# A two-layer decoder trunk on one core: gate and up products through DRAM scratch, weight parts for two chunks, and weight sums made by accumulating transfers

## The chip, the cores and the metric

The kernel runs on one core of a Trainium2 chip. The metric is the device time of one execution in microseconds (us), lower is better. The core has a matrix engine (TensorE, "PE" in the profile), a vector engine (VectorE, "DVE"), a scalar engine (ScalarE, "ACT"), GpSimd ("POOL") and SyncE ("SP"), which here only issues transfers. Every engine works through its own instructions in order and waits on semaphores for the others. Sixteen DMA engines move the data that SP, ACT and POOL ask for.

## The reference, cut to what matters

Two layers work on 512 positions of 1024 features. Each has a mixer (attention with forget gates and a short convolution in the first, a gated linear recurrence in the second), a cross attention into 256 memory rows, and a SwiGLU block. Each part has the form x = x + norm(f(norm(x))). The change touches the SwiGLU block, whose width is 2816:

```python
D_FF = ((8 * D_MODEL // 3 + 255) // 256) * 256       # 2816
def swiglu(h, w_gu, w_down):
    g, u = jnp.split(h @ w_gu, 2, axis=-1)
    return (jax.nn.silu(g) * u) @ w_down
...
        h = rmsnorm(x, g_ffn_pre[layer])
        y = swiglu(h, w_ffn_gu[layer], w_ffn_down[layer])
        x = x + rmsnorm(y, g_ffn_post[layer])
```

Everything is float32.

## The kernel before, in words

**Split operands.** A float32 product is made from three matmuls of a rounded kind (`mm3`, L278). Each operand is split in a high part, a copy in the rounded type made by ACT, and a low part, the difference, made by DVE (`split_out`, L427, with the two instructions at L430 and L431). The three matmuls are high by high, high by low, low by high (L279 to L281). So each weight tile has to be loaded by SP (`load_raw`, L117), cast on ACT and subtracted on DVE before PE can use it.

**Buffers.** A buffer is a slot of a pool. `gpool` has 14 groups of 128 x 2048 elements. The raw weights (tag "st"), the high parts ("wh") and the low parts ("wl") have four buffers each of 128 x 1024 elements. Eight small buffers of 516 columns serve everything else of that kind (`sbuf`).

**The block.** `ffn` (L717) works in chunks of 256 columns of the weights, eleven for the gate and eleven for the up half. The first of each (`ws_gemm_split`, L334) is a plain product, woven with the end of the cross attention; its instructions go over the first 256 positions and then over the second. The other ten pairs use a Winograd form of the Strassen product (class `Winograd`, L353): the activations are cut into four blocks, by positions (halves) and by features (halves), the weight chunk into four blocks as well, and seven products replace eight. The activation side (`__init__`, L360) makes four sums once, splits them and keeps them in four groups "wa"; three further products use parts of the transposed activations, the groups "hTh" and "hTl", directly.

**The weight side** (`weights`, L381) runs for every chunk. It loads the upper half of the rows, r0, and the lower half, r1, each 128 x 4 x 256. Four sums on DVE at L384 make a third tile tt, a small tile t2, and overwrite half of r0. Then four splits follow: r0 (for the products "b11" and "t1"), t2, tt ("t4" and "t3") and r1 ("b21" and "b22"). With r0, r1 and tt a chunk holds three of the four "st" buffers, and its splits take four "wh" and four "wl".

**Products and outputs.** `gemm` (L396) runs the seven products in the order a11 b11, s2 t2, n1 t1, n3 t3, a12 b21, a22 t4, n4 b22, each 4 x 3 matmuls of 256 columns, 84 in all, and combines the results on DVE (L411, and through `out` L741 and L746). The gate chunk writes to one half of the PSUM banks and gets a Silu on ACT (L743); the up chunk uses the other half, and its result times the gate's is y (L748). Each pair of chunks makes 128 x 2 x 512 elements of y. Two pairs share a group "y2", so six groups hold all of y.

**The down projection** (`OutProj`, L439) contracts the 22 blocks of y with `w_ffn_down`. Its first half (`half0_steps`, L458) goes through the blocks two at a time: `parts` (L754) splits a pair's y, called two steps ahead, and a load and split of two weight rows follow. The second half (`half1`) uses the same split y again.

**What sets the order.** PE's instructions run as written. On the other engines and queues, the planner of the framework orders the instructions when the program is built: by program order as priority, by the time at which it reckons that inputs and buffers are there. It also places every wait. What it puts on one engine or queue runs in that order on the chip. SP's queue carries all weight loads; POOL's carries small work of the norms (the power at L210, `rstd`) and a few transfers.

Of the kernel before, what the change touches and what calls it, by code (L numbers as in the profile page):

```python
# [42 lines left out]
def trunk_kernel(ctx: ExitStack, tc: tile.TileContext, a: dict, out: bass.AP):  # L43
# [207 lines left out]
    def new_hT():  # L251
# [3 lines left out]
        ft.ghi, ft.glo, ft.raw = hi, lo, None  # L255
        return ft

    def put_T(hT, t, hs, bank=bankB):
        for hf in range(2):
            ps = bank()  # L260
            for j in range(4):
                nc.tensor.transpose(
                    out=ps[:, j * P:(j + 1) * P], in_=hs[hf][:, j * P:(j + 1) * P], identity=ident
                )
            v = ps.rearrange("p (k c) -> p k c", k=4)
            sl = slice(t * P, (t + 1) * P)
            if hT.raw:
                nc.scalar.copy(out=hT.raw[hf][:, :, sl], in_=v)
            last = (
                nc.scalar.copy(out=hT.ghi[hf][:, :, sl], in_=v).ins,  # L270
                nc.vector.tensor_tensor(
                    out=hT.glo[hf][:, :, sl], in0=v, in1=f(hT.ghi[hf][:, :, sl]), op=ALU.subtract
                ).ins,
            )
        return last

# [57 lines left out]
    def ws_gemm_split(w, c0s, hT, hook):  # L334

        wss = [w_chunk(w, c0) for c0 in c0s]
        banks = [[bankA() for _ in range(2)] for _ in c0s]
        for half in range(2):
            cols = slice(half * 256, half * 256 + 256)
            for i, ws in enumerate(wss):  # L340
                for m in range(2):
                    for kh in range(2):
                        wh, wl = ws[kh]
                        for kk in range(4):
                            k = 4 * kh + kk
                            ms = slice(m * P, (m + 1) * P)
                            mm3(banks[i][m][:, cols], wh[:, kk, ms], wl[:, kk, ms],
                                hT.hi[k][:, cols], hT.lo[k][:, cols], k == 0, k == KT - 1)
                    if half == 0:
                        hook(2 * i + m)  # L350
        return banks

    class Winograd:  # L353
# [6 lines left out]
        def __init__(self, hT):  # L360
            r0, r1 = hT.raw
            e, l = slice(0, 256), slice(256, 512)
            a21, a11, a22, a12 = r0[:, :, e], r0[:, :, l], r1[:, :, e], r1[:, :, l]
            sub = lambda o, i0, i1: nc.vector.tensor_tensor(out=o, in0=i0, in1=i1, op=ALU.subtract)
            self.parts = {}
            sub(a22, a21, a22)
            sub(a21, a21, a11)
            sub(a11, a11, a22)
            for name, raw in (("s2", a11), ("n1", a22), ("n3", a21)):
                self.put(name, raw)  # L370
            sub(a12, a12, a11)
            self.put("n4", a12)
            for name, hf, sl in (("a11", 0, l), ("a12", 1, l), ("a22", 1, e)):
                self.parts[name] = hT.ghi[hf][:, :, sl], hT.glo[hf][:, :, sl]

        def put(self, name, raw):
            g = group("wa")
# [1 line left out]
            split_out(raw, *self.parts[name])  # L379

        def weights(self, w, c0):  # L381
            r0, r1 = load_raw(w, 0, 4, c0, 256), load_raw(w, 4, 4, c0, 256)
            one, two = slice(0, P), slice(P, 2 * P)
            add = lambda o, i0, i1: nc.vector.tensor_tensor(out=o, in0=i0, in1=i1, op=ALU.add)  # L384
            t2 = sbuf("t2").rearrange("p (k c) -> p k c", k=4)
            tt = wst.tile([P, 4, 256], F32, tag="st", name="st")
            add(tt[:, :, two], r0[:, :, two], r1[:, :, two])
            add(t2, tt[:, :, two], r0[:, :, one])
            add(r0[:, :, two], r0[:, :, one], r0[:, :, two])
            add(tt[:, :, one], t2, r1[:, :, one])  # L390
            w1, w2 = split_w(r0, 4, 256), split_w(t2, 4, P)
            w3, w4 = split_w(tt, 4, 256), split_w(r1, 4, 256)
            return {"b11": (w1, one), "t1": (w1, two), "t2": (w2, one), "t4": (w3, one),
                    "t3": (w3, two), "b21": (w4, one), "b22": (w4, two)}

# [321 lines left out]
    def ffn(layer, hT, prev, proj):  # L717
        w = a["w_ffn_gu"][layer]
        y = Feat([None] * NFF, [None] * NFF)

        y2 = {}

        def y_rows(jp):

            if jp % 2 == 0:
                y2[jp // 2] = f(group("y2"))
            return y2[jp // 2][:, jp % 2 * 2:jp % 2 * 2 + 2, :]

        def act(jp, gb, ub):
            y_ = y_rows(jp)  # L730
            for m in range(2):
                s = sbuf("sw")
                nc.scalar.activation(out=s, in_=gb[m], func=AF.Silu)
                nc.vector.tensor_tensor(out=y_[:, m, :], in0=s, in1=ub[m], op=ALU.mult)

        def act_wino(jp, wino):

# [12 lines left out]
            wino.gemm(w, jp * 256, bankB, gate)  # L750
            y_ = y_rows(jp)
            wino.gemm(w, FF + jp * 256, bankA, up)

        def parts(jp):  # L754
# [388 lines left out]
    for layer in range(2):  # L1143
# [49 lines left out]
```

## Time and profile before

| | |
|---|---|
| median of three runs | 1481.75 us (1480.46 to 1481.83) |
| the profiled execution | 1479.13 us |
| its span, first to last instruction | 1477.3 us |
| granted TensorE clock | 0.998 |
| bytes moved | 151.26 MB, 102 GB/s over the span |
| weight loads of the gate and up stage | 88 of 512 KB |
| the weight sums at L384 | 160, from 383.0 to 1339.4 us |

In the rows of the profile a name such as wl<-st,wh tells what is written from what is read, by the program's names for tiles; t is the small sum t2, y also stands for the groups y2. A row of a group ends with the busy time, the mean of one in ns, and the idle time of the engine just before these instructions with what ended most of it. In a row of waits the engine that waited stands left of the arrow, what it waited for on the right. A row of single instructions begins with its start and its duration in us, and ends with the idle time before it, in brackets, where there was some. Matmuls overlap, so their single durations add up to more than PE's busy time.

### The profile page before, as it was taken

The numbers are of one execution on the slowest core, as the hardware profiler recorded it, in microseconds if no ns is written. First come the engines' busy times: TensorE is split into PE (matmuls) and PEld (weight loads), VectorE is DVE, ScalarE is ACT, GpSimd is POOL, SyncE is SP. The second block draws the span as 40 slices with busy tenths as digits, with TensorE's granted clock in tenths as the row PEclk, the third lists the DMA queues.
The fourth block names the chain that finished last, engine by engine and source line by source line (L and its number), as shares of the span: only waits on it lengthen the run. The fifth ranks groups of instructions, "written<-read, shape, count | busy, mean of one in ns | idle before, by whom it ended". The sixth has DMA issues, their size and how long they took to land. (4 is left out here: it accounts for less than half of the span.)

```text
span 1477.3 us, 21423 instructions
## 1 busy us (share of the span) xinstructions
PE 1423.2 (96%) x8564; PEld 1254.8 (85%) x8564; DVE 1021.3 (69%) x1623; ACT 660.8 (45%) x1069; POOL 37.6 (3%) x82
## 2 busy tenths in 40 slices
PE   8999999999998899999999999999999999989998
PEld 6777789888898888888889888988889888888886
DVE  5785767544888888883447998744588888888232
ACT  4354555434553433461334886543464333345130
POOL 1000000000100000000000000000010000000000
PEclk9999999999999999999999999999999999999999
DMA  5532253520322323233413236342122232234221
GB/s 174 180 100 79 79 178 108 163 75 23 112 72 86 100 86 101 86 126 115 156 53 94 86 100 193 124 155 72 31 85 72 86 96 92 86 100 130 99 86 57
DMA packets 119391, 151.26 MB, mean 102 GB/s; under 512 B 6182, under 2 KB 88178, under 8 KB 119291
## 3 DMA queue, kind: packets, MB, share of 16 engines
q1 hardware_dynamic: 114722, 140.92, 30.3%
q10 hardware_dynamic: 3896, 6.86, 1.6%
q0 software_dynamic: 672, 2.11, 0.4%
q8 instruction: 67, 1.10, 0.3%
q14 instruction: 34, 0.27, 0.1%
HBM read 147.76 MB, written 2.11 MB: 101 GB/s over the span
## 5 line engine op out<-in xcount | busy, mean ns | idle before, releaser
L431 DVE TENSOR_TENSOR wl<-st,wh 128x1024 fp32r<-128x1024 f32 x268 | 324.1, 1223 | 225.2 <-ACT wh L430 223.2
L430 ACT CAST wh<-st 128x1024 fp32r<-128x1024 f32 x268 | 277.9, 1050 | 425.2 <-DVE st L384 193.9
L279 PE MATMUL bA<-hTh,wh 128*128 128x256 f32 (+1 forms) x816 | 275.8, 338 | 0.0
L281 PE MATMUL bA<-hTh,wl 128*128 128x256 f32 (+1 forms) x816 | 272.3, 334 | 0.6 <-DVE wl L431 0.6
L280 PE MATMUL bA<-hTl,wh 128*128 128x256 f32 (+1 forms) x816 | 271.8, 333 | 0.0
L281 PEld LDWEIGHTS bA<-hTh,wl 128*128 128x128 f32 x816 | 154.9, 190 | 16.5 <-DVE wl L431 1.0
L280 PEld LDWEIGHTS bA<-hTl,wh 128*128 128x128 f32 x816 | 155.2, 190 | 13.7
L279 PEld LDWEIGHTS bA<-hTh,wh 128*128 128x128 f32 x816 | 155.1, 190 | 13.5
L281 PE MATMUL bB<-wa,wl 128*128 128x256 f32 x320 | 92.4, 289 | 22.8 <-DVE wl L431 22.8
L279 PE MATMUL bA<-wa,wh 128*128 128x256 f32 x320 | 92.5, 289 | 12.7 <-ACT wh L430 12.7
L281 PE MATMUL bA<-wa,wl 128*128 128x256 f32 x320 | 92.6, 289 | 4.5 <-DVE wl L431 4.5
L279 PE MATMUL bB<-wa,wh 128*128 128x256 f32 x320 | 90.5, 283 | 0.0
L280 PE MATMUL bB<-wa,wh 128*128 128x256 f32 x320 | 90.4, 283 | 0.0
L280 PE MATMUL bA<-wa,wh 128*128 128x256 f32 x320 | 90.4, 283 | 0.0
L281 PEld LDWEIGHTS bB<-wa,wl 128*128 128x128 f32 x320 | 61.2, 191 | 26.4 <-DVE wl L431 26.4
L456 PE MATMUL bB<-wh,y 128*128 128x512 f32 x208 | 81.1, 390 | 1.3 <-DVE y L431 1.3
L454 PE MATMUL bB<-wh,y 128*128 128x512 f32 x208 | 81.2, 390 | 1.1 <-ACT y L430 1.1
L455 PE MATMUL bB<-wl,y 128*128 128x512 f32 x208 | 80.9, 389 | 0.0
L279 PEld LDWEIGHTS bA<-wa,wh 128*128 128x128 f32 x320 | 61.2, 191 | 16.7 <-ACT wh L430 16.7
L281 PEld LDWEIGHTS bA<-wa,wl 128*128 128x128 f32 x320 | 61.2, 191 | 8.6 <-DVE wl L431 8.6
L281 PE MATMUL bB<-hTh,wl 128*128 128x256 f32 x240 | 68.0, 283 | 0.0
L279 PE MATMUL bB<-hTh,wh 128*128 128x256 f32 x240 | 67.9, 283 | 0.0
(289 smaller groups left out, 3143.4 us busy)
## 6 DMA issues: line engine op xcount, KB each, us to landing
st<-in_w_ffn_gu_dram SPq DMA_DIRECT2D x88, 512.0 KB, 3.5
st<-in_w_ffn_down_dram SPq DMA_DIRECT2D x44, 512.0 KB, 3.9
st<-in_w_xkv_dram SPq DMA_DIRECT2D x32, 512.0 KB, 5.0
st<-in_ab_w_in_dram SPq DMA_DIRECT2D x24, 512.0 KB, 3.7
st<-in_w_xq_dram SPq DMA_DIRECT2D x16, 512.0 KB, 3.5
st<-in_w_xo_dram SPq DMA_DIRECT2D x16, 512.0 KB, 3.8
st<-in_c_w_in_dram SPq DMA_DIRECT2D x16, 512.0 KB, 3.5
st<-in_ab_w_out_dram SPq DMA_DIRECT2D x8, 512.0 KB, 3.8
```

Source lines behind the costliest of these rows:

```text
L279: nc.tensor.matmul(out=ps, lhsT=wh, rhs=xh, start=first, stop=False)
L280: nc.tensor.matmul(out=ps, lhsT=wh, rhs=xl, start=False, stop=False)
L281: nc.tensor.matmul(out=ps, lhsT=wl, rhs=xh, start=False, stop=last)
L430: nc.scalar.copy(out=hi, in_=src)
L431: nc.vector.tensor_tensor(out=lo, in0=src, in1=f(hi), op=ALU.subtract)
L454: nc.tensor.matmul(out=ps, lhsT=yh, rhs=wh[:, kk, :], start=first, stop=False)
L455: nc.tensor.matmul(out=ps, lhsT=yh, rhs=wl[:, kk, :], start=False, stop=False)
L456: nc.tensor.matmul(out=ps, lhsT=yl, rhs=wh[:, kk, :], start=False, stop=last)
```

## The change

Five things change together.

- The sums of r0 with itself and of r0 with r1 are no longer made by DVE. A load on SP puts the block b12 into tt; an accumulating transfer on POOL adds b22 to it from DRAM, and another adds b11 to the second half of r0. The sums for t2 and for the first half of tt stay on DVE.
- r0 and r1 are loaded into one group, "wr", and their splits go to two groups, "wg". The splits of t2 and tt still use "wh" and "wl", of which a chunk now takes two each; of the "st" buffers it takes one.
- The products y go to a scratch tensor in DRAM, y2, written by SP (`put_y`) from an "st" buffer at the end of each pair, and read back into one by `parts` in the down projection.
- The transposed activations of this block are held in four groups by halves of features and of positions ("quads"), each with high and low parts, in place of two high and two low groups over all positions.
- `put_T` and `ws_gemm_split` address these quads through two small functions.

```diff
+    def new_quads():
+
+        ft = Feat(None, None)
+        ft.quads = [[group("hTq") for _ in range(2)] for _ in range(2)]
+        ft.raw = None
+        return ft
+
+    def dst_T(hT, hf, t):
+        if hT.hi:
+            sl = slice(t * P, (t + 1) * P)
+            return hT.ghi[hf][:, :, sl], hT.glo[hf][:, :, sl]
+        q, c = hT.quads[hf][t // 2], t % 2 * P
+        return q[:, :, c:c + P], q[:, :, 256 + c:256 + c + P]
+
+    def half_T(hT, k, half):
+        if hT.hi:
+            cols = slice(half * 256, half * 256 + 256)
+            return hT.hi[k][:, cols], hT.lo[k][:, cols]
+        q = hT.quads[k // 4][half][:, k % 4, :]
+        return q[:, 0:256], q[:, 256:512]
...
-            for name, hf, sl in (("a11", 0, l), ("a12", 1, l), ("a22", 1, e)):
-                self.parts[name] = hT.ghi[hf][:, :, sl], hT.glo[hf][:, :, sl]
+            for name, hf, half in (("a11", 0, 1), ("a12", 1, 1), ("a22", 1, 0)):
+                q = hT.quads[hf][half]
+                self.parts[name] = q[:, :, 0:256], q[:, :, 256:512]
...
         def weights(self, w, c0):
-            r0, r1 = load_raw(w, 0, 4, c0, 256), load_raw(w, 4, 4, c0, 256)
+            raw = f(group("wr")).rearrange("p a (b c) -> p (a b) c", c=256)
+            rows = w.rearrange("(k p) n -> p k n", p=P)
+            r0, r1 = raw[:, 0:4, :], raw[:, 4:8, :]
+            for kh, r in ((0, r0), (4, r1)):
+                nc.sync.dma_start(out=r, in_=rows[:, kh:kh + 4, c0:c0 + 256])
             one, two = slice(0, P), slice(P, 2 * P)
             add = lambda o, i0, i1: nc.vector.tensor_tensor(out=o, in0=i0, in1=i1, op=ALU.add)
             t2 = sbuf("t2").rearrange("p (k c) -> p k c", k=4)
-            tt = wst.tile([P, 4, 256], F32, tag="st", name="st")
-            add(tt[:, :, two], r0[:, :, two], r1[:, :, two])
+            tt = wst.tile([P, 4, 256], F32, tag="st", name="tt")
+
+            def split_g(r):
+                g = group("wg").rearrange("p a (b c) -> p (a b) c", c=256)
+                split_out(r, g[:, 0:4, :], g[:, 4:8, :])
+                return g[:, 0:4, :], g[:, 4:8, :]
+
+            nc.sync.dma_start(out=tt[:, :, two], in_=rows[:, 0:4, c0 + P:c0 + 2 * P])
+            nc.gpsimd.dma_start(out=r0[:, :, two], in_=rows[:, 0:4, c0:c0 + P], accum_op=ALU.add)
+            nc.gpsimd.dma_start(out=tt[:, :, two], in_=rows[:, 4:8, c0 + P:c0 + 2 * P], accum_op=ALU.add)
             add(t2, tt[:, :, two], r0[:, :, one])
-            add(r0[:, :, two], r0[:, :, one], r0[:, :, two])
             add(tt[:, :, one], t2, r1[:, :, one])
-            w1, w2 = split_w(r0, 4, 256), split_w(t2, 4, P)
-            w3, w4 = split_w(tt, 4, 256), split_w(r1, 4, 256)
+            w1, w2 = split_g(r0), split_w(t2, 4, P)
+            w3, w4 = split_w(tt, 4, 256), split_g(r1)
...
-        y2 = {}
+        y2 = dram.tile([P, NFF, 512], F32, name=f"y2_{layer}")
+        yraw = {}
 
         def y_rows(jp):
 
-            if jp % 2 == 0:
-                y2[jp // 2] = f(group("y2"))
-            return y2[jp // 2][:, jp % 2 * 2:jp % 2 * 2 + 2, :]
+            yraw[jp] = wst.tile([P, 2, 512], F32, tag="st", name="yr")
+            return yraw[jp]
+
+        def put_y(jp):
+            nc.sync.dma_start(out=y2[:, 2 * jp:2 * jp + 2, :], in_=yraw[jp])
...
             y_ = y_rows(jp)
             wino.gemm(w, FF + jp * 256, bankA, up)
+            put_y(jp)
 
         def parts(jp):
             yg = group("y")
-            src = y2[jp // 2][:, jp % 2 * 2:jp % 2 * 2 + 2, :]
+            src = wst.tile([P, 2, 512], F32, tag="st", name="yr")
+            nc.sync.dma_start(out=src, in_=y2[:, 2 * jp:2 * jp + 2, :])
             split_out(src, yg[:, 0:2, :], yg[:, 2:4, :])
...
-        hTf = new_hT()
+        hTf = new_quads()
```

More of the change, by code (lines that the diff above doesn't have):

```diff
@@ L268, in put_T @@
                 nc.scalar.copy(out=hT.raw[hf][:, :, sl], in_=v)
+            hi, lo = dst_T(hT, hf, t)
             last = (
[L270 to L273, printed above, removed]
+                nc.scalar.copy(out=hi, in_=v).ins,
+                nc.vector.tensor_tensor(out=lo, in0=v, in1=f(hi), op=ALU.subtract).ins,
             )
@@ L347, in ws_gemm_split @@
                             mm3(banks[i][m][:, cols], wh[:, kk, ms], wl[:, kk, ms],
-                                hT.hi[k][:, cols], hT.lo[k][:, cols], k == 0, k == KT - 1)
+                                *half_T(hT, k, half), k == 0, k == KT - 1)
                     if half == 0:
@@ L752, in act_wino @@
             wino.gemm(w, FF + jp * 256, bankA, up)
+            put_y(jp)
         def parts(jp):
             yg = group("y")
-            src = y2[jp // 2][:, jp % 2 * 2:jp % 2 * 2 + 2, :]
+            src = wst.tile([P, 2, 512], F32, tag="st", name="yr")
+            nc.sync.dma_start(out=src, in_=y2[:, 2 * jp:2 * jp + 2, :])
             split_out(src, yg[:, 0:2, :], yg[:, 2:4, :])
```

## The prediction

> **What bounds the kernel now.** I read the page's totals and its forty slices first, then a table of busy time in stretches, then the waits of the two stages that the change touches, then single instructions inside them.
>
> ```profile
> PE 1423.2 (96%) x8564; PEld 1254.8 (85%) x8564; DVE 1021.3 (69%) x1623; ACT 660.8 (45%) x1069; POOL 37.6 (3%) x82
> PE   8999999999998899999999999999999999989998
> DVE  5785767544888888883447998744588888888232
> DMA  5532253520322323233413236342122232234221
> ```
>
> TensorE (PE) is busy for 96% of the span, so 1477.3 - 1423.2 = 54 us is all that a change that leaves its matmuls alone can win. VectorE (DVE) runs at 8 tenths in two stretches, slices 10 to 17 and 29 to 36. These are the gate and up products of the two layers. In the table of stretches (columns: busy time and instructions of PE, weight load, DVE, ACT, POOL, then clock, DMA share, GB/s) I cut them into pieces of 23.33 us, which is one gate chunk plus one up chunk:
>
> ```profile
> 456.67:480.00 23.33, 20.91 (x168) 20.30 (x168) 19.64 (x31) 9.25 (x14) 0.00 (x0) 1.00 0.30 92
> 596.67:620.00 23.33, 21.19 (x173) 20.59 (x172) 19.51 (x31) 9.26 (x14) 0.00 (x0) 1.00 0.31 95
> 1203.33:1226.67 23.34, 21.20 (x173) 20.59 (x172) 19.63 (x31) 9.30 (x13) 0.00 (x0) 1.00 0.32 96
> 660.00:690.00 30.00, 30.00 (x134) 24.86 (x133) 14.39 (x13) 8.25 (x9) 0.00 (x0) 1.00 0.42 130
> ```
>
> Every pair loses 2.1 to 2.4 us of PE. Ten pairs in each of two layers make about 40 of the 54 us. The last row is the down projection: PE is full there. What PE waits for is in the waits of 370 to 640 us (first seven rows) and of 1060 to 1340 us (last three); columns are total, times, longest:
>
> ```profile
> ACT wh L430 <- DVE st L384: 97.1, 19, 5.8
> DVE wl L431 <- ACT wh L430: 18.3, 29, 2.4
> PE bB L281 <- DVE wl L431: 11.5, 9, 1.4
> PE bA L279 <- ACT wh L430: 5.7, 9, 0.7
> PE bA L281 <- DVE wl L431: 2.3, 10, 0.3
> SPq L119 <- DVE wx L411: 74.8, 16, 5.2
> SPq L119 <- DVE t L384: 66.4, 9, 7.4
> ...
> PE bB L281 <- DVE wl L431: 11.3, 9, 1.3
> PE bA L279 <- ACT wh L430: 5.7, 9, 0.7
> PE bA L281 <- DVE wl L431: 2.3, 10, 0.3
> ```
>
> (The two SPq rows are the transfer queue's own waits from 456 to 640 us.) PE waits for split weights only: 11.5 + 5.7 + 2.3 = 19.5 us in layer 0 and 11.3 + 5.7 + 2.3 = 19.3 us in layer 1, together 38.8 us. The casts wait for the weight sums of L384, and the loads wait for buffers that DVE has yet to release. One pair in single instructions:
>
> ```profile
> 480.02 0.38 PE L279 MATMUL bA<-wa,wh 128*128 128x256 f32 x1 [0.65 <-ACT wh L430]
> 480.75 0.39 PE L281 MATMUL bA<-wa,wl 128*128 128x256 f32 x1 [0.22 <-DVE wl L431]
> 492.61 0.39 PE L281 MATMUL bB<-wa,wl 128*128 128x256 f32 x1 [1.38 <-DVE wl L431]
> ...
> 485.46 0.68 DVE L384 TENSOR_TENSOR t<-st 128x512 f32<-128x512 f32 x1
> ...
> 490.67 1.29 DVE L748 TENSOR_TENSOR y<-y,sw 128x512 f32<-128x512 f32 x2
> 491.87 0.69 DVE L431 TENSOR_TENSOR wl<-t,wh 128x512 fp32r<-128x512 f32 x1
> ...
> 488.14 0.62 ACT L430 CAST wh<-t 128x512 fp32r<-128x512 f32 x1
> ```
>
> The late part is always the t2 weight of the second product: its low part at 491.87 us stands in DVE's queue behind the outputs of the chunk before, and PE goes on when it ends (491.87 + 0.69 = 492.56). DVE does 19.6 us in order in 23.3 us, with weights ready hardly ahead of their use.
>
> **The change, part by part.** 1. *Two sums fewer on DVE.* Each chunk makes four L384 sums; the change leaves t2 and tt.one.
>
> ```profile
> L384 DVE TENSOR_TENSOR st<-st x80: 680/685/694, 383.0 to 1332.8; 128x512 f32<-128x512 f32 x80
> ...
> L431 DVE TENSOR_TENSOR wl<-st,wh 128x1024 fp32r<-128x1024 f32 x268 | 324.1, 1223 | 225.2 <-ACT wh L430 223.2
> L430 ACT CAST wh<-st 128x1024 fp32r<-128x1024 f32 x268 | 277.9, 1050 | 425.2 <-DVE st L384 193.9
> ```
>
> The 80 st<-st are the removed ones (minimum, median, maximum in ns); the two page rows give the cast and the low part that every weight part needs. 80 x 0.685 = 54.8 us leave DVE, four per pair, 2.7 us: DVE goes from 19.6 to about 16.9 us per pair, 80% of PE's 21.2. DVE isn't the bound in itself; what this buys is room in its queue.
>
> 2. *Depth.* Before, wh and wl have four buffers and a chunk uses all four, and a chunk takes three of the four st buffers. Afterwards the two full parts of r0 and r1 go to the groups "wg", the raw weights to a group "wr", and t2 and tt alone take wh and wl, so four buffers hold two chunks. The groups suffice: of 14, three quads and four wa stay, 7 are left, and a chunk needs 3. The quad of a21, first half, is dead after the split products at the start, and the six groups of y2 are gone. A whole chunk (10.6 us of PE) of lead outweighs a stall of at most 1.4 us at a time. So the waits above go, except where there is no lead yet: the first chunks after the start of each layer, where DVE also makes the four wa parts. I leave 1 us per layer. Gain: 38.8 - 2 = 36.8 us.
>
> 3. *Transfers in place of the sums.* Per chunk they are one more load of 256 KB on SP and two accumulating ones of 256 KB on POOL; each is 128 x 4 rows of 512 B, so 512 packets. The trace has no accumulating transfer. The nearest rows (landing is the last column; the queue rows are of 456 to 480 us and, last, of 660 to 720 us):
>
> ```profile
> st<-in_w_ffn_gu_dram SPq DMA_DIRECT2D x88, 512.0 KB, 3.5
> cb<-cum POOLq DMA_DIRECT2D x8, 256.0 KB, 3.7
> L930 POOL DMA_DIRECT2D cb<-cum x8: 546/548/778, 66.0 to 147.3; - x8
> DMA to landing us min/median/max: 3.3/3.7/5.0
> q1 hardware_dynamic: 2112, 2.10, 28.2%
> q1 hardware_dynamic: 3536, 6.82, 36.5%
> ```
>
> The first queue row gives 0.282 x 24 x 16 engines / 2112 = 51 ns of an engine per packet of 1 KB, the second 0.365 x 60 x 16 / 3536 = 99 ns per 2 KB: time goes by bytes, so 512 B is some 26 ns. For an accumulating packet the low end is that, 26 ns; the high end is three whole 1 KB packets (read the source, read the target, write), 154 ns; I take 51 ns, two reads of 512 B, nearest to the row of 1 KB. Per pair: r0 and r1 2048 x 51 / 16 = 6.5 us; the tt loads 1024 x 26 / 16 = 1.7; the accumulating 2048 x 51 / 16 = 6.5 (3.3 to 19.7); the write of y 256 x 99 / 16 = 1.6. Sum 16.3 us of 21.2, from 13.1 to 29.5. So the engines keep up, at three quarters instead of 30%.
>
> The Trainium skill (DMA: Bandwidth & Descriptors, section "SDMA does more than copy") has the add unit combine two streams; two streams of 512 B would be my 51 ns, and no run here shows it yet. Against the change speaks its rule in "Rules for kernel authors" to make transfers of at least 1 MiB: by its fit of 2.0 us plus bytes over 436 GB/s a quarter MiB is 2.6 us, and with four accumulates one behind the other that would be an estimated 10.4 us per pair, still under PE's 21.2. The trace's own 256 KB transfer from POOL has 3.7 us.
>
> POOL issues 128 rows in 0.55 us; 512 rows take 0.55 to 2.2, four per pair 2.2 to 8.8 us of 21.2 on an engine that does nothing in this stage. Latency of the longest chain: load 3.5, issue up to 2.2, accumulate 3.7 to 5.0, cast 1.05, low part 1.22: 11.7 to 13 us. Raw weights of the chunk after next fit while a chunk runs, which is a lead of one to two chunks, 10.6 to 21 us. Cost 0; with the cover gone, each chunk waits for what is over.
>
> 4. *Products through DRAM.* Eleven writes and eleven reads of 512 KB per layer, all on SP's queue.
>
> ```profile
> out_dram<-x SPq DMA_DIRECT2D x8, 256.0 KB, 2.1
> st<-in_w_ffn_down_dram SPq DMA_DIRECT2D x44, 512.0 KB, 3.9
> 651.62 0.50 PE L454 MATMUL bB<-wh,y 128*128 128x512 f32 x1 [0.53 <-ACT y L430]
> 653.01 0.50 PE L456 MATMUL bB<-wh,y 128*128 128x512 f32 x1 [0.66 <-DVE y L431]
> ```
>
> The write waits for L748 on SP; behind it stand loads of chunks that PE wants a chunk later, so 0. A read per step of the down projection doubles the st buffers and bytes of half 0: 512 packets of 2 KB by 99 ns over 16 is 3.2 us in a step of 24 matmuls, 30.00 x 24 / 134 = 5.4 us. Landing 3.9, cast and low part 2.3 are 6.2 us per buffer, and four buffers over 6.2 us give 0.65 per us against 2 / 5.4 = 0.37 wanted. Hidden, too. The first reads ask for pairs 0 and 1, which were written over 200 us before; cost 0. If they had to wait for the last write: L748 0.69, write 2.1 to 3.9, read 3.9, cast and low part 2.3, 9 to 11 us after the last product, less the 1.2 us that PE waits there now, so 8 to 10 us per layer, 16 to 20 us. That is kept for the range.
>
> 5. *Quads and POOL's queue.* The split of each transposed tile is the same two instructions to other columns; 0. On POOL, the norms' power (L210) can stand behind an accumulate that waits for its load, at most 3.5 us per layer in the first chunk; I take 0 since PE has 24 us of split products there, and keep 7 us for the range.
>
> **Sum.** The profiled execution took 1479.13 us (span 1477.3), 2.6 us under the median 1481.75. 1479.1 - 36.8 = 1442.3, and 2.6 on top for the median makes 1445 us, 2.5% faster. With all 38.8 + 2 x 1.2 us of waits gone it is 1440.6. Runs differ by some 1.4 us, so the low end is 1438.
>
> **Rivals.** *A: accumulating transfers become the bound (slower).* Place: the 16 DMA engines in the gate and up stage. They decide once an accumulating packet costs more than (21.2 - 9.8) x 16 / 2048 = 89 ns; from (23.33 - 9.8) x 16 / 2048 = 106 ns the kernel is slower than before. At the 154 ns end a pair takes 29.5 us: 20 x (29.5 - 23.33) = +123 us, 1605 us; at 120 ns it takes 25.2 us, +37 us, 1519 us. For it: nothing in the trace prices such a packet. Against: the packets that it does show go by bytes.
>
> *B: the reads wait for the last write.* +16 to 20 us on the forecast, 1461 to 1465 us. For it: nothing shows how finely the order of transfers to the scratch tensor is kept. Against: the first reads name other rows of the scratch tensor than the last write.
>
> *C: the stalls are an order, not a depth.* The late low part of t2 was behind output instructions of DVE; its sum had been made at 485.46 us, six us before. If DVE's order keeps t2 behind those outputs, only the shorter queue helps: half of the waits, say 19 us, remain, 1464 us; with late accumulates ahead of DVE in addition nothing is won, 1482 us, and the change does not do what it says. For it: that row. Against: the cast it followed was at 488.14, limited by a chain that is now a chunk earlier.
>
> **How the numbers follow.** Forecast (1438 to 1453) 0.62; B or C with part of the gain (1453 to 1478) 0.15; C without gain 0.05; A or another loss 0.18. A difference of 0.2%, 3 us, is what a measurement of this kernel can tell from none. Faster 0.77, same 0.05, slower 0.18. The range goes from 1438 to 1488: forecast, B, C and the mildest part of A, about 0.82. The forecast's own range is 1438 to 1453.
>
> **What would show it.** Right: PE at 21 us of 21.2 to 21.6 per pair, no row of PE waiting for wl or wh beyond a few us, 40 and 40 L384 instead of 160, DVE near 80%, DMA share near 0.75 in the stage. Step 3 is wrong if ACT or DVE waits on transfers of gate and up weights stand at tens of us, or if the POOL transfers land after 10 us or more; A, if the DMA share is 9 tenths and PE's waits end in them. Step 4 is wrong if PE waits 8 us or more at the first matmul of the down projection. C, if PE's waits for wl are still there with weights long landed. My forecast falls if a pair takes more than 22 us.

## The result, and the profile after

The changed kernel takes 1597.41 us (median; 1592.17 to 1600.45). The kernel before, run beside it on the same chip, takes 1481.11 us (1479.89 to 1481.83). The ratio is 1.0782, with a 95% interval of 1.0748 to 1.0817: 7.8% slower, where 2.5% faster was forecast. The profiled execution has a span of 1598.1 us, 120.8 us more than the 1477.3 of before.

The page's totals and slices:

```profile
PE 1472.3 (92%) x8564; PEld 1297.9 (81%) x8564; DVE 984.8 (62%) x1543; ACT 663.5 (42%) x1069; POOL 140.1 (9%) x162
PE   9999999999887878779999999999998787877998
PEclk9999999999988999979999999999998899998999
```

PE has the same 8564 matmuls, yet it is busy 49 us longer (1472.3 against 1423.2), and its share fell to 92%. Both dips, in slices 11 to 18 and 31 to 37 (about 400 to 720 us and 1200 to 1480 us), are the gate and up stages and the start of the down projections. There the clock row dips too; before, it stood at 9 throughout. The table of stretches (span, busy time and instructions of PE, weight load, DVE, ACT, POOL, then clock, DMA share, GB/s) shows one pair in the first row, the next pair and 0.7 us more in the second, and 8 us at the head of the first pair in the others (in stretches as short as these a DMA share can come out above 1):

```profile
541.14:569.44 28.30, 23.36 (x169) 22.53 (x169) 17.37 (x27) 9.04 (x12) 5.31 (x5) 0.91 0.68 149
569.44:597.74 28.30, 23.20 (x170) 22.18 (x171) 18.04 (x27) 9.72 (x13) 5.37 (x5) 0.94 0.70 158
...
541.00:543.00 2.00, 1.86 (x7) 1.64 (x8) 1.53 (x3) 1.13 (x2) 1.12 (x1) 0.50 0.97 279
543.00:545.00 2.00, 2.00 (x11) 2.00 (x11) 0.49 (x1) 0.00 (x0) 0.00 (x0) 0.50 1.16 245
545.00:547.00 2.00, 2.00 (x14) 2.00 (x13) 0.00 (x0) 0.44 (x1) 0.00 (x0) 0.67 0.43 53
547.00:549.00 2.00, 2.00 (x19) 2.00 (x18) 1.36 (x2) 1.56 (x2) 0.00 (x0) 1.00 0.00 0
```

This pair takes 28.30 us. In the kernel before, a pair of 168 matmuls takes 23.06 us; the prediction's pieces of 23.33 us held up to 173. DVE does what was predicted for it, about 17 us of work, and is now idle for ten. PE is idle for 28.30 - 23.36 = 4.9 us, and the 23.36 us are stretched: in the five us behind the stall the granted clock is 0.50, and 2 us hold 11 matmuls instead of 19. The largest waits of PE in the whole run (total, times, longest) say where it stands still:

```profile
PE bB L299 <- ACT wh L462: 68.9, 20, 4.1
PE bB L486 <- ACT wh L462: 19.1, 2, 9.9
PE bA L299 <- ACT wh L462: 14.9, 20, 2.5
PE bA L301 <- DVE wl L463: 5.7, 20, 0.8
```

The first row is the second product of each gate chunk (bank bB), 3.4 us in the mean, once per pair; the second is the first matmul of the two down projections; the last two are the up chunks. One stall in single instructions (start, duration, engine, line; idle time before and what ended it in brackets):

```profile
538.37 0.68 DVE L782 TENSOR_TENSOR yr<-bA,wy 128x512 f32<-128x512 f32 x1
539.09 0.69 DVE L784 TENSOR_TENSOR yr<-yr,sw 128x512 f32<-128x512 f32 x1
539.70 0.68 DVE L409 TENSOR_TENSOR t<-tt,wr 128x512 f32<-128x512 f32 x1
...
540.47 0.62 ACT L462 CAST wh<-t 128x512 fp32r<-128x512 f32 x1 [2.66 <-DVE t L409]
...
541.14 0.58 PE L299 MATMUL bB<-wa,wh 128*128 128x256 f32 x1 [3.80 <-ACT wh L462]
```

PE had finished the gate chunk's first product at 541.14 - 3.80 = 537.34. DVE then does the last outputs of the pair before, to 539.78, and only behind them the sum t2 of the chunk that PE is already in; its cast follows, and PE goes on when that ends, at 541.09. In the kernel before, the sum and the cast of t2 were done before the outputs, and only the low part stood behind them. Not all of the 3.80 us is the order, though: the two accumulating transfers into a tt at this place were issued at 531.33 and 532.2 us and landed 5.4 to 5.9 us later, at 536.7 to 538.1. From then on the sum could have run, 1.6 to 3.0 us before it did.

At the down projection, first SP's queue, then PE:

```profile
702.78 0.32 SPq L762 DMA_DIRECT2D y<-yr  x1
703.20 0.37 SPq L794 DMA_DIRECT2D yr<-y  x1
703.91 0.50 SPq L119 DMA_DIRECT2D st<-in_w_ffn_down_dram  x1
...
710.50 0.80 PE L486 MATMUL bB<-wh,y 128*128 128x512 f32 x1 [9.21 <-ACT wh L462]
```

The first down weight is issued behind the write of the last pair, with one read between, and that write waits for the pair's last output. PE waits 9.21 us here, and its clock is 0.50 behind that wait too:

```profile
712.00:716.00 4.00, 4.00 (x10) 3.17 (x11) 2.90 (x3) 2.09 (x2) 0.00 (x0) 0.50 0.85 267
```

The account of the 120.8 us: from the second product of the first of the ten pairs to that of the last, nine pairs take 254.8 us in layer 0 and 251.5 in layer 1 (27.2 to 32.5 each), against 9 x 23.08 = 207.7 each before, 90.9 us more. The rest of the last pair takes about 3.4 us more in both layers together. The first waits of the two down projections are 20.0 us against 2.4, 17.6 more. Half speed behind them, until 717.0 and about 1474.7 us, costs about 6. That is 118; the rest lies elsewhere.

The accumulating transfers, on the page and from 541 to 569 us (queue: packets, MB, share of 16 engines; issue: count, KB, median us to landing):

```profile
q0 software_dynamic: 2112, 1.05, 30.7%
wr<-in_w_ffn_gu_dram POOLq DMA_DIRECT2D x40, 256.0 KB, 5.0
tt<-in_w_ffn_gu_dram POOLq DMA_DIRECT2D x40, 256.0 KB, 5.5
```

0.307 x 28 us x 16 / 2112 = 65 ns of an engine per packet. These are four transfers, so one goes in 528 packets. They land after 5.0 and 5.5 us.

### The profile page after: what moved, and what is told of

Read it like the earlier page. It is cut to its first block, busy times and chain, and to the rows that moved or that the text cites. A ratio compares the mean times of both kernels' runs of the same rounds, so it can differ in the third digit from the quotient of the medians.

```text
span 1598.1 us, 21738 instructions
## 1 busy us (share of the span) xinstructions
PE 1472.3 (92%) x8564; PEld 1297.9 (81%) x8564; DVE 984.8 (62%) x1543; ACT 663.5 (42%) x1069; POOL 140.1 (9%) x162
## 3 DMA queue, kind: packets, MB, share of 16 engines
q0 software_dynamic: 42912, 23.09, 11.2%
## 4 chain that ended last, share of the span: by engine, by line
PE 77%; DMA 10%; DVE 8%; issue 2%; ACT 2%; SPq 0%; POOL 0%; POOLq 0%; DVEq 0%; ACTq 0%
PE bA L301 10%; PE bA L299 10%; PE bA L300 10%; DMA wr<-in_w_ffn_gu_dram 8%; PE bB L487 4%; PE bB L488 4%; PE bB L486 4%; PE bA L488 4%; PE bA L486 4%; PE bA L487 4%; PE bB L301 4%; PE bB L299 4%; PE bB L300 4%; DVE wg L463 2%; ACT wg L462 1%
## 5 line engine op out<-in xcount | busy, mean ns | idle before, releaser
L463 DVE TENSOR_TENSOR wl<-st,wh 128x1024 fp32r<-128x1024 f32 x148 | 180.6, 1222 | 189.7 <-ACT wh L462 188.5
L462 ACT CAST wh<-st 128x1024 fp32r<-128x1024 f32 x148 | 155.4, 1051 | 217.8 <-PE bA L300 68.6
L299 PE MATMUL bA<-hTh,wh 128*128 128x512 f32 (+1 forms) x448 | 171.4, 383 | 0.0
L301 PE MATMUL bA<-hTh,wl 128*128 128x512 f32 (+1 forms) x448 | 168.0, 375 | 0.0
L300 PE MATMUL bA<-hTl,wh 128*128 128x512 f32 (+1 forms) x448 | 167.7, 374 | 0.0
L463 DVE TENSOR_TENSOR wg<-wr,wg 128x1024 fp32r<-128x1024 f32 x80 | 96.2, 1221 | 112.5 <-ACT wg L462 112.5
L462 ACT CAST wg<-wr 128x1024 fp32r<-128x1024 f32 x80 | 80.3, 1046 | 183.2 <-DMA wr<-in_w_ffn_gu_dram 175.2
L299 PE MATMUL bB<-wa,wh 128*128 128x256 f32 x160 | 57.2, 358 | 68.9 <-ACT wh L462 68.9
L301 PEld LDWEIGHTS bA<-hTh,wl 128*128 128x128 f32 x448 | 84.3, 188 | 15.5
L486 PEld LDWEIGHTS bB<-wh,y 128*128 128x128 f32 x208 | 40.3, 194 | 28.0 <-ACT wh L462 19.5
L299 PE MATMUL bA<-wa,wh 128*128 128x256 f32 x160 | 48.3, 302 | 14.9 <-ACT wh L462 14.9
```

Source lines behind the costliest of these rows:

```text
L299: nc.tensor.matmul(out=ps, lhsT=wh, rhs=xh, start=first, stop=False)
L300: nc.tensor.matmul(out=ps, lhsT=wh, rhs=xl, start=False, stop=False)
L301: nc.tensor.matmul(out=ps, lhsT=wl, rhs=xh, start=False, stop=last)
L462: nc.scalar.copy(out=hi, in_=src)
L463: nc.vector.tensor_tensor(out=lo, in0=src, in1=f(hi), op=ALU.subtract)
L486: nc.tensor.matmul(out=ps, lhsT=yh, rhs=wh[:, kk, :], start=first, stop=False)
```

## The experiments

Times are medians, ratios against the kernel before on the same chip. "After" is the changed kernel.

**e1_plain: after, with the two accumulating transfers made plain copies.** The additions are left out: what lands replaces what was there. The order of all engines is that of after.

```diff
-  nc.gpsimd.dma_start(out=r0[:, :, two], in_=..., accum_op=ALU.add)
-  nc.gpsimd.dma_start(out=tt[:, :, two], in_=..., accum_op=ALU.add)
+  nc.gpsimd.dma_start(out=r0[:, :, two], in_=...)
+  nc.gpsimd.dma_start(out=tt[:, :, two], in_=...)
```

> The changed kernel with the 80 accumulating transfers made plain copies of the same size and place (so the second half of r0 and of tt are not the sums; the order of every queue and engine is unchanged). Theory 1 (queue order): the stall of 4 us at the second product of every gate chunk comes from where the tt loads and the POOL transfers stand in their queues, behind loads of the next chunk that wait for PE to release a group; adding or copying hardly matters: 1570 to 1600 us, stalls of over 3 us at each pair stay. Theory 2 (the accumulating packet): its 65 ns against some 30 for a copy and its landing of 5 us are what is late: a copy lands in 3 to 3.7 us, most of the stalls and the half-clock stretches behind them go, 1500 to 1530 us.

1584.66 us, ratio 1.071 (1.0689 to 1.0732). Accumulating instead of copying is worth 13 us of the 116 lost. That can be more than the adding alone: as plain copies the same transfers go in 80 packets each instead of 528. The stall of each gate chunk stays: 56.8 us in 20 waits, longest 4.0, against 68.9.

**e2_sums_dve: after, with all four sums back on DVE.** No transfer adds; the deep buffers and the products in DRAM stay.

```diff
-  (the tt load, both accumulating transfers)
+  add(tt[:, :, two], r0[:, :, two], r1[:, :, two])
   add(t2, tt[:, :, two], r0[:, :, one])
+  add(r0[:, :, two], r0[:, :, one], r0[:, :, two])
```

> The changed kernel with all four sums back on DVE; groups wr and wg, products through DRAM and quads stay. No tt load and no POOL transfer is left. Both theories take the gate and up stalls of 4 us away; the depth of two chunks then shows its own worth. If depth alone does what the prediction said, PE loses under 0.5 us per pair: 1479 - 39 plus 2 x 13 us lost at the start of the down projection, about 1465. If weights stay just in time because DVE has 19.6 us in 21.2, about 1500.

1617.67 us, ratio 1.0934 (1.0918 to 1.0951), slower still. Single instructions of one stall:

```profile
509.80 2.59 SPq L407 DMA_DIRECT2D wr<-in_w_ffn_gu_dram  x4
...
535.10 0.42 DVE L781 TENSOR_TENSOR yr<-bA,wx 128x256 f32<-128x256 f32 x1 [2.46 <-PE bA L301]
...
538.18 0.68 DVE L783 TENSOR_TENSOR yr<-yr,sw 128x512 f32<-128x512 f32 x1
538.78 0.68 DVE L409 TENSOR_TENSOR wr<-wr 128x512 f32<-128x512 f32 x1
...
540.64 0.58 PE L299 MATMUL bB<-hTq,wg 128*128 128x256 f32 x1 [4.14 <-ACT wg L461]
```

The weights of this chunk were asked for from 509.80 to 512.39 us, over 20 us before their sums; by the median of this run a load of this shape lands after 5.6. Nothing on the way of the data is late, and DVE even idles for 2.46 us ahead of the outputs: the sums stand among and behind the outputs (L781, L783) in its order, and PE pays 4.14 us.

**e3_st6_g13: after, with six weight buffers instead of four, and 13 groups instead of 14.**

```diff
-G = 14
+G = 13
-WS = 4
+WS = 6
```

> The changed kernel with six st buffers instead of four and 13 groups instead of 14 (the same SBUF). Theory 1, with the four st buffers that tt shares with the products as the reason for tt's late place: tt gets its buffer a pair earlier, the 4 us stalls shrink to under 1.5 us and the half clock goes: 1460 to 1510 us. Theory 2: the landing times stay, and so do the stalls: 1580 to 1600 us.

1679.74 us, ratio 1.1354 (1.1337 to 1.1371). More room for weights made it slower by another 82 us: the stalls of the gate chunks stay (71.5 us in 20 waits), and those of the up chunks grow from 14.9 to 43.6 us. So it isn't a lack of weight buffers that makes the gate chunks wait. What of the 82 us is the group taken away wasn't separated.

**e4_dram_only: before, with only the products going through DRAM.** As in the change, each pair's product stands in a weight buffer until it is written.

```diff
-  y2[jp // 2] = f(group("y2"))
+  yraw[jp] = wst.tile([P, 2, 512], F32, tag="st", name="yr")
...
+  put_y(jp)     (write to DRAM on SP; parts() reads back)
```

> The kernel before with one part of the change: the products go through DRAM, held in st buffers, nothing else. Theory 1: the products take one of four st buffers in the gate and up stage, where a chunk holds three, so loads start later there and PE waits more than 2.1 us per pair; and at the down projection the first weight load stands behind the last product write: together +25 us or more, above 1506 us. Rival (the transfer of the products is hidden, as predicted): 1475 to 1490 us.

1630.79 us, ratio 1.1019 (1.1001 to 1.1038): this part alone costs 151 us, more than the whole change, and far more than I had thought of. Two rows of DVE and one of PE:

```profile
539.39 0.69 DVE L752 TENSOR_TENSOR yr<-yr,sw 128x512 f32<-128x512 f32 x1
540.00 0.69 DVE L384 TENSOR_TENSOR st<-st 128x512 f32<-128x512 f32 x1
...
543.28 0.39 PE L279 MATMUL bB<-hTh,wh 128*128 128x256 f32 x1 [4.65 <-ACT wh L430]
```

Here all four sums of the gate chunk stand behind the last output (L752), so even the first product waits. The chunk's loads were late too, but less: the second was issued at 531.70 us, after a wait for a buffer, and by the run's median of 3.6 us it landed some 4.7 us before the first sum. From here on the theory was: what costs is the place of a chunk's sums and low parts in DVE's order, behind the outputs of the pair before, and the half clock that follows a wait of that length. The rival was the traffic itself.

**e5_dram_group: e4_dram_only, but the product stands in a group buffer until it is written.** Same transfers, same queue.

```diff
-  yraw[jp] = wst.tile([P, 2, 512], F32, tag="st", name="yr")
+  yraw[jp] = f(group("yr"))[:, 0:2, :]
```

> The kernel before with its products kept in DRAM scratch and nothing else changed, as in the run e4_dram_only, but a product stands in one of the 14 group buffers until it is written, not in one of the four weight buffers. VectorE's order is then the one of the kernel before (the next gate chunk's sums ahead of the outputs of the pair), the traffic to DRAM is that of e4_dram_only (1630.79 us). Theory of the order (the gate chunk stalls because its sums stand behind the outputs of the pair before on VectorE, and the clock halves after such a stall): stalls at the head of a gate chunk 1.5 us or less, clock 1.00 in the stage, about 1495 us (1475 to 1515), what is over 1480 being the start of the down projection. Rival, the traffic (the write and the read in the queue hold the loads, wherever the product stands): 1580 or more, the stalls of 4 us still there.

1488.83 us, ratio 1.0059 (1.0042 to 1.0076). With the traffic unchanged, 142 us are gone. PE's waits from 440 to 640 us:

```profile
PE bB L281 <- DVE wl L431: 11.5, 9, 1.4
PE bA L279 <- ACT wh L430: 5.2, 8, 0.7
```

The first is that of the kernel before (11.5, 9 times, longest 1.4). The rival falls: writing and reading back 11.5 MB is nearly free, and holding the product in the weight buffers is what costs, here where a chunk takes three of the four. The 9 us left lie outside these waits; 4 of them are at the start of the down projections, where the first matmuls wait 6.4 us in all against 2.4.

**e6_accum_only: before, with only the two accumulating transfers.**

```diff
-  add(tt[:, :, two], r0[:, :, two], r1[:, :, two])
+  (tt load on SP, two accumulating transfers on POOL)
   add(t2, tt[:, :, two], r0[:, :, one])
-  add(r0[:, :, two], r0[:, :, one], r0[:, :, two])
```

> The kernel before with two of the four sums made by accumulating transfers and nothing else changed: four weight buffers, so little lead, and products stay in SBUF. Theory of the order: VectorE's written order has the chunk's last sum and low parts behind two or three of the pair's outputs, so a stall of 2 to 3 us is left at each gate chunk, with half a clock behind it where it is over 3 us: 1500 to 1570. Rival, the accumulating transfers as the bound: 1580 or more, with stalls that end at the landing of an accumulating transfer. If neither holds, under 1490, and the accumulating transfers are harmless even without the lead.

1556.14 us, ratio 1.0518 (1.0503 to 1.0534). The number is in the range of the order, the reason is not. DVE's waits and one of them:

```profile
DVE t L384 <- DMA tt<-in_w_ffn_gu_dram: 93.5, 24, 5.8
...
502.84 0.69 DVE L384 TENSOR_TENSOR t<-tt,st 128x512 f32<-128x512 f32 x1 [5.10 <-DMA tt<-in_w_ffn_gu_dram]
```

The sum t2 waits for the landing of the transfer, 24 times and 93.5 us in all, and the outputs wait behind it. Without lead, the chain of load and accumulate is longer than the cover; this is step 3's "each chunk waits for what is over". It wasn't a bound on packets: the queue's share is the 11.5% that it has in after (11.2%).

**e7_ahead: after, with each chunk's loads, sums and splits written one chunk earlier.** Transfers, buffers and traffic stay.

```diff
-  wino.gemm(w, jp * 256, bankB, gate)
+  ready.append(wino.weights(w, FF + jp * 256))
+  wino.gemm(ready.pop(0), bankB, gate)
   y_ = y_rows(jp)
-  wino.gemm(w, FF + jp * 256, bankA, up)
+  if jp + 1 < NFF // 2:
+      ready.append(wino.weights(w, (jp + 1) * 256))
+  wino.gemm(ready.pop(0), bankA, up)
```

> The changed kernel, but each chunk's weight loads, sums and splits are written one chunk earlier, before the products of the chunk ahead of it, so that a gate chunk's sums and low parts stand ahead of the outputs of the pair before on VectorE. Transfers, buffers and traffic are those of the changed kernel. Theory of the order: stalls at the head of a gate chunk under 1 us, clock 0.97 or more in the stage, a pair in 21.5 to 23.5 us instead of 28.2, so about 1597 - 20 x 5.5 = 1487 us (1455 to 1510). Rival, the traffic or the queues: stalls of 3 us or more stay, 1560 or more.

1482.14 us, ratio 1.0018 (1.0004 to 1.0032): 115 us back from one move in the order in which the program is written. Of the 20 waits for the second product's cast two short ones are left, 1.5 us together; 14 others, 2.8 us at most, are for a copy (L444) that stands on ACT behind a cast whose raw weight is late. PE's two largest waits, and such a cast, 0.95 us ahead of the copy:

```profile
PE bB L299 <- ACT wx L444: 19.2, 14, 2.8
PE bB L485 <- ACT wh L461: 19.2, 2, 9.9
...
516.29 1.04 ACT L461 CAST wg<-wr 128x1024 fp32r<-128x1024 f32 x1 [6.67 <-DMA wr<-in_w_ffn_gu_dram]
```

**e8_sums_ahead: e2_sums_dve, written one chunk earlier in the same way.**

> As e7_ahead (weights written one chunk earlier), but all four sums on VectorE as in e2_sums_dve (1617.67 us). Theory of the order: the stall goes here too; VectorE then has some 19.6 us of work in a pair, so 1480 to 1520 us, and what lies between this run and e7_ahead is what the two accumulated sums are worth (0 to 25 us). Rival, the traffic or the queues: 1580 or more.

1459.05 us, ratio 0.9861 (0.9846 to 0.9876): 1.4% faster than before, 159 us faster than e2_sums_dve, with the same instructions and transfers. The stretch of 480 to 600 us, and the row of PE that is left:

```profile
480.00:600.00 120.00, 120.00 (x997) 119.63 (x997) 111.57 (x178) 52.59 (x71) 0.00 (x0) 1.00 0.40 128
...
640.92 0.79 PE L484 MATMUL bB<-wh,y 128*128 128x512 f32 x1 [9.24 <-ACT wh L460]
```

PE is full at clock 1.00, a pair of 168 matmuls in 20.2 us, with DVE at 93% and all four sums on it. So in this stretch PE has none of the waits that the depth of the change was to take away, once the order uses it; and taking two sums off DVE can win nothing there.

**e11_ahead_plain: e7_ahead, with plain copies for the accumulating transfers.** The additions are left out, as in e1_plain.

> e7_ahead (1482.14 us) with its accumulating transfers made plain copies, so that the additions are left out; order, buffers and bytes asked for are those of e7_ahead. If what e7_ahead loses to e8_sums_ahead (23 us) is the addition in the transfer, under 1468 us. If it is the chain of a further load of small packets behind the first, whatever it does on landing, 1474 to 1486.

1460.32 us, ratio 0.9869 (0.9854 to 0.9884), 22 us less than e7_ahead and within 2 us of e8_sums_ahead. So it is the accumulating that costs, not one more load in the chain. What of it is the addition and what the packets (528 a transfer against 80) isn't separated. From 480 to 600 us, e7_ahead:

```profile
480.00:600.00 120.00, 112.39 (x896) 110.67 (x896) 88.32 (x137) 48.28 (x66) 26.85 (x21) 0.97 0.81 184
```

and e11_ahead_plain:

```profile
480.00:600.00 120.00, 119.38 (x987) 118.42 (x986) 98.68 (x153) 52.29 (x70) 17.23 (x23) 1.00 0.67 208
```

The kernel gets less far in the first stretch (896 matmuls against 987), and per matmul the engines move about as much in both. For that they are busier with accumulating transfers: 0.81 at 184 GB/s against 0.67 at 208.

**e9_write_pool: e8_sums_ahead, with the products' write issued by POOL.**

```diff
-  nc.sync.dma_start(out=y2[...], in_=yraw[jp])
+  nc.gpsimd.dma_start(out=y2[...], in_=yraw[jp])
```

> e8_sums_ahead (1459.05 us) with the write of a pair's products issued by POOL instead of SP. Theory of the queue (the first down weight is late because the write of the last pair, which waits for the pair's last output, stands in front of the reads and the down weights in SP's queue): the wait at the start of the down projection falls from 9.7 us to 3 to 6 us in each of the two layers, 1446 to 1454 us. Rival, the buffers (reads and down weights wait for the four weight buffers, whichever queue the write is in): the wait stays above 8 us, 1456 to 1462.

1453.95 us, ratio 0.9821 (0.9806 to 0.9836). 5 us won, in the range of the queue, but the wait itself only fell from 9.24 to 8.21 us (one row for each, the down projection of layer 0), as the rival had it. SP's waits from 600 to 640 us, and DVE at that place:

```profile
SPq L119 <- DVE y L461: 15.7, 1, 15.7
...
628.60 0.69 DVE L784 TENSOR_TENSOR yr<-yr,sw 128x512 f32<-128x512 f32 x1
629.21 3.49 DVE L461 TENSOR_TENSOR y<-yr,y 128x1024 fp32r<-128x1024 f32 x3
```

The first down weight now waits 15.7 us for a weight buffer. A read of products holds it until its low part is made, and the low parts of the first three reads stand behind the last output on DVE. It is the order once more; SP's write was the smaller part of the delay.

**e10_reads_early: e9_write_pool, with the first two reads of products and their splits written before the last up chunk.**

```diff
   if jp + 1 < NFF // 2:
       ready.append(wino.weights(w, (jp + 1) * 256))
+  else:
+      parts(0)
+      parts(1)
```

> e9_write_pool, and the first two reads of products from DRAM with their splits are written before the last up chunk, so that the first down weight is the next but one to ask for a weight buffer. Theory of the order: the wait at the start of the down projection goes below 2 us in both layers and the clock stays at 1.00 there, so e8's 1459 less two times 9.7 us of wait and 2.5 to 3.5 us of half clock: 1433 to 1437 us (1428 to 1443). Rival, the DMA engines are full there and the first weights land late all the same: 1446 or more.

1444.94 us, ratio 0.9762 (0.9749 to 0.9775), 9 us won, and 2 us above the range of the order. DVE, then PE:

```profile
630.04 0.69 DVE L784 TENSOR_TENSOR yr<-yr,sw 128x512 f32<-128x512 f32 x1
631.79 1.22 DVE L461 TENSOR_TENSOR wl<-st,wh 128x1024 fp32r<-128x1024 f32 x1
...
633.06 0.50 PE L485 MATMUL bB<-wl,y 128*128 128x512 f32 x1 [3.62 <-DVE wl L461]
```

The first weight is loaded and cast in time now, so the wait moved from its high part (L484) to its low part (L485): that still stands behind the last outputs and a split of a read product. The next expectation puts this wait down to the second weight's late load; the row says that it is the low part of the first.

**e12_last_kept: e10_reads_early, with the last pair's product kept in a group buffer,** neither written nor read back, so that a weight buffer more is free; the low parts of the first two down weights then stand ahead of the last outputs on DVE.

```diff
+  if jp == NFF // 2 - 1:
+      yraw[jp] = f(group("yr"))[:, 0:2, :]
+  else:
       yraw[jp] = wst.tile([P, 2, 512], F32, tag="st", name="yr")
```

> e10_reads_early (1444.94 us) with the products of the last pair of a layer kept in a group buffer, neither written to DRAM nor read back, so that one of the four weight buffers more is free at the end of the stage; on VectorE the low parts of the first two down weights then stand ahead of the last outputs. Theory of the buffers (the second down weight of e10 was issued 12 us after the first read because it waited for a weight buffer that a read of products held until its split, behind the last outputs): the two waits of 3.6 us and the half clock behind them go, 1432 to 1438 us. Rival, the splits of the reads themselves are late (VectorE and ScalarE have more to do at that place than PE covers): waits of 2 us or more stay there under another name, 1441 to 1447.

1433.23 us, ratio 0.9687 (0.9674 to 0.97): 3.1% faster than the kernel before and 10% faster than the changed one. The page's totals:

```profile
PE 1411.6 (99%) x8564; PEld 1255.1 (88%) x8564; DVE 1013.7 (71%) x1623; ACT 660.3 (46%) x1069; POOL 48.3 (3%) x102
```

PE is busy for 1411.6 us of 1430.8, and the down projection starts without a wait (620 to 640 us: PE 20.00, clock 1.00):

```profile
620.00:640.00 20.00, 20.00 (x126) 18.11 (x126) 13.00 (x17) 9.26 (x11) 0.00 (x0) 1.00 0.61 190
```

## Why the prediction was wrong, point by point

**What bounds the kernel: right.** It named PE's waits for late split weights as what is to be won, 38.8 of 54 us of idle time. e12_last_kept wins 46 us over before, and of those waits only 3.3 us per layer are left, for the first of the ten pairs; the prediction had left 1.

**Step 1, two sums fewer on DVE: right in size, worth nothing.** 80 instructions went, and DVE's pair is 17.4 us against a predicted 16.9. But e8_sums_ahead keeps all four sums and fills PE: DVE's load was never the limit.

**Step 2, depth: this is the step that failed.** It said that a whole chunk of lead outweighs stalls of 1.4 us, "so the waits above go". The lead was counted in buffers. DVE does its instructions in their order, and there the sum of t2 was behind the outputs of the pair before: the wait became outputs, sum and cast one behind the other, 3.8 us instead of 1.4. e2_sums_dve shows it with weights asked for 20 us ahead; e8_sums_ahead, the same work written a chunk earlier, takes this wait away. In e8_sums_ahead PE is full from 480 to 600 us, as this step had it. Which part of the change moved the sums behind the outputs isn't shown in the changed kernel itself: the accumulating was taken out of it, and the stalls stayed (e1_plain, e2_sums_dve). e4_dram_only and e5_dram_group point to the place of the products.

**Step 3, accumulating transfers: bounds right, "cost 0" wrong.** 65 ns per packet instead of 51, inside 26 to 154 and under the 89 ns at which rival A was to decide. With the load's share beside it, a pair has 0.69 x 28.30 = 19.5 us of transfers against 16.3 forecast. In a pair of 28.30 us accumulating costs 13 us over the run (e1_plain); against a PE that needs 20.2 us it hides less, and costs 22 us (e7_ahead less e11_ahead_plain). The prediction's own sign for a wrong step 3 was there as well: ACT's casts waited 175.2 us, in 34 waits, for the transfers into wr.

**Step 4, products through DRAM: wrong twice.** "So 0" looked at when the write is issued, and at four buffers in the down projection. It did not look at what a product held in the weight buffers does to the order in the gate and up stage: e4_dram_only less e5_dram_group, 142 us. Why the program's planner puts the sums behind the outputs in that case was not tried on the chip; that the place of the product decides it there is shown. In the changed kernel, where a chunk takes one weight buffer and not three, no run moved the products of all pairs elsewhere. The write, in SP's queue ahead of the first down weights, was one part of the 9.21 us at the start of the down projection; the larger was the weight buffers that the reads hold until their low parts, which stand behind the last outputs on DVE (e9_write_pool, e10_reads_early, e12_last_kept). The bound kept in the range, 16 to 20 us for both layers, was the right size.

**Step 5: nothing seen against it.** POOL's issues take 1.27 us for 512 rows (median of 40), inside the 0.55 to 2.2 given.

**The rivals.** A was not the cause: e1_plain is still 105 us above the kernel before. B's price came, not its reason: two reads were issued at 680.62 us, 22 us before the last write. C was the mechanism, "the stalls are an order, not a depth", and its row was quoted; but it was allowed to take away the gain and no more (1482 us at most). It didn't ask what else can move behind the outputs, and it didn't have the clock. Its test, waits with weights long landed, was the right one, and e2_sums_dve is that case. The chance of 0.18 for slower was too low because only A was worked out as a loss.

**What no step had: the clock.** In the mean of eighteen pairs, PE is idle for 4.9 of 28.1 us and busy for 23.2, where the kernel before needs 20.9 at full clock for the same matmuls. That is 2.3 us more per pair, 45 us over twenty pairs, for running at half speed behind the stalls. A stall of 3.8 us costs about 6.

## What to carry to other kernels

Depth in buffers is worth only what the order of each engine lets it be: before counting lead in buffers, read for every engine in order what stands ahead of the late instruction, and write the preparation of the next chunk ahead of the outputs of this one. A buffer pool that two kinds of data share is part of that order: a result parked among the weight buffers moved the sums, and cost 142 us that the same result in another pool did not. And price a wait of TensorE with the clock behind it: 1.4 us cost 1.4, 3.8 us cost about 6.

## What the runs showed of the hardware that was not expected

**The clock.** Behind the wait of 3.80 us the granted clock was half for five us (rows above); in the kernel before, behind a wait of 1.38 us at 492.61, it stayed whole:

```profile
494.00:496.00 2.00, 2.00 (x19) 2.00 (x18) 2.00 (x4) 0.00 (x0) 0.00 (x0) 1.00 0.01 2
```

In e6_accum_only a wait of 1.42 us, ending at 504.29, and the start of the next were enough. The clock fell at 505.0, before that second wait of 1.86 us had ended at 506.65:

```profile
502.00:504.00 2.00, 0.87 (x8) 0.66 (x6) 1.16 (x3) 0.38 (x1) 0.11 (x1) 1.00 0.62 76
506.00:508.00 2.00, 1.35 (x6) 1.35 (x7) 2.00 (x3) 1.22 (x3) 0.00 (x0) 0.50 0.39 130
510.00:512.00 2.00, 2.00 (x12) 2.00 (x11) 1.47 (x2) 0.03 (x1) 0.10 (x1) 0.55 0.72 213
```

Read in stretches of a quarter us, the clock of the changed kernel falls twelve times from 400 to 720 us, at 539.5, 570.2 and 597.5 among others. The falls lie 5, 5, 8, 8, 8, 9, 8, 8, 8, 8 and 7 times 3.41 us apart, and the clock stays low for 3.4 us seven times, 6.8 four times and 13.7 once. So here it changes only at steps of 3.41 us, and what a stall costs depends on where in a step it lies. In the 3.41 us ahead of a fall PE was idle for 1.8 to 3.3 us, in e6_accum_only at 505.0 for only 1.6. The kernel before, whose waits in this stage are 1.4 us at most, has no fall from 380 to 640 us.

The Trainium skill (TensorE: Matmul & The Clock Gate, section "What's actually happening") has the half rate after an idle window of about 3.4 us, and the full rate again after about as long of sustained work. The steps of 3.41 us agree with its length; that the window has to be idle as a whole doesn't agree, since 1.6 us of idle time were enough.

**The add in a transfer.** An accumulating packet of 512 B takes 65 ns of an engine where 51 were taken from the row of 1 KB packets. A plain copy of 256 KB issued by POOL goes in 80 packets, an accumulating one in 528 (queue rows of 541 to 569 us in e1_plain and in after: 320 and 2112 packets for four transfers). Plain copies of the same 256 KB land after 3.7 and 4.5 us in e11_ahead_plain, accumulating ones after 4.7 and 6.2 us in e7_ahead, behind the same queues:

```profile
wr<-in_w_ffn_gu_dram POOLq DMA_DIRECT2D x40, 256.0 KB, 4.7
tt<-in_w_ffn_gu_dram POOLq DMA_DIRECT2D x40, 256.0 KB, 6.2
```
